# A hybrid encoder block: streamed tiles moved by 32 bytes, decay tables filled up to 128 rows, and two heads' score products in turns

## The chip, the core and the metric

The kernel runs on one core of one Trainium2 chip. The metric is the device time of one execution in microseconds (us). The median of the runs shown is what a change is measured against. TensorE does the products, VectorE (DVE), ScalarE (ACT) and GpSimd (POOL) the elementwise work, SyncE (SP) issues most transfers.

## What is computed

One layer of a two-branch encoder block over 1024 tokens of 1024 features, in float32. The part that the change touches is the chunked SSD scan: 16 heads of 64 channels, 8 chunks of 128 tokens, forward and backward.

```python
h = _rms_norm(x, norm_mix_pre); proj = h @ w_in
z, xbc, dt_raw, u = jnp.split(proj, split_at, axis=-1)
y_ssd = _ssd_mixer(z, xbc, dt_raw, ...)          # two directions of _ssd_scan, then gate and norm
y_s5 = _s5_mixer(u, ...)                          # S5 scan, then g * sigmoid(g @ glu_w + glu_b)
mix = jnp.concatenate([y_ssd, y_s5], axis=-1) @ w_out
x = x + _rms_norm(mix, norm_mix_post)
h = _rms_norm(x, norm_ffn_pre)
f = (jax.nn.silu(h @ w_gate) * (h @ w_up)) @ w_down
x = x + _rms_norm(f, norm_ffn_post)
...
# in _ssd_scan, per head and chunk (l, s: tokens of a chunk)
decay = jnp.exp(jnp.where(lower, a_cum[..., :, None] - a_cum[..., None, :], -jnp.inf))
scores = jnp.einsum("bclgn,bcsgn->bcgls", cc, bc)
y_diag = jnp.einsum("bcgrls,bcsgrp->bclgrp", scores[:, :, :, None] * decay, xdt)
y_off = jnp.einsum("bclgn,bcgrpn,bcgrl->bclgrp", cc, states_in, jnp.exp(a_cum))
```

## The kernel before

The large products are done in float32r halves: an operand is split into a high and a low part, and three products (high by high, high by low, low by high) are added in PSUM. In the profile a product is written `out<-streamed,stationary`. The stages, in the order of the program: norm and the input projection (streamed `hTh`, `hTl`), the S5 branch, the GLU of the S5 branch (streamed `gh`, `glo`, function `gemm`, L271), the SSD branch, the output projection (streamed `ohi`, `olo`, L1123), the gate and up products of the feed-forward in Winograd's form (streamed `B` and `T`, L1535), the down product (streamed `dop`, L1839).

The SSD branch works on eight units `q`, each of two heads; a unit has two halves `hf` of four chunks. It is written as a generator, and pieces of it are let in between the pieces of the GLU and of the output projection (`fill_with`). Outside the stretches with a manual schedule, priorities set the order in which a scheduler places instructions on each engine; each engine then runs its list in order. In one half of a unit:

- `u3`: for each head and direction the exponents of the decay are made on TensorE. A product of `ra` (streamed) with `la` (stationary), both of 16 rows (L971), and a product of `neg` with `idr` of 128 rows that adds the mask (L972) fill one PSUM bank; ACT takes the exponential into `E`. Two more products of `ra` with `efs`, over 8 rows (L978), give the factors `EF`. Eight units by two halves by four make 64 products of 16 rows, and there are 32 of 8 rows.
- `u4`: `M` of a head is the sum of its two `E` times the scores `SL` (L990, L991). The products of `M` with `X` (L994, float32, 64 stationary columns) put head 0 in partitions 0 to 63 of `yd` and head 1 in 64 to 127: four products of head 0, then four of head 1. Each is two passes in the profile. DVE and POOL then add the part from the chunk states (L1008, L1011 to L1013).

The first rows of `la` and the last of `ra` are constants made once by `ssd_tables`; the other eight rows are loaded for each unit (`unit_loads`). `t16`, `r16`, `dtT` and `xT` take turns in two buffers of the tag `xT`.

SBUF is given out from both ends. In the kernel before, the tiles of the pools on the right side start 32 bytes past a multiple of 64, and so do those behind `dvec` on the left: `gh`, `glo`, `ohi`, `olo`, `T`, `ra`, `neg`, `M`, `CT`, `Xw` among the streamed ones. `hTh`, `hTl`, `B` and `dop` start at multiples of 64.

Of the kernel before, what the change touches and what calls it, by code (L numbers as in the profile page):

```python
# [18 lines left out]
def _ap(t, off, dims):  # L19
    """A free-dimension pattern over all partitions of tile t."""  # L20
    return bass.AP(tensor=t.tensor, offset=t.offset + off, ap=[list(t.ap[0])] + [list(d) for d in dims])
# [109 lines left out]
def hymba_block(ctx, tc, P, out, dbg=None, upto=99):  # L131
# [69 lines left out]

# [1 line left out]
    ident = const.tile([128, 128], F32, name="ident")  # L203
# [13 lines left out]

# [1 line left out]
    wst = ctx.enter_context(tc.tile_pool(name="wst", bufs=2))  # L219
# [31 lines left out]
    def ensure(i):  # L251
        """splits of the weight blocks up to i, and the load of the one after"""
        for j in range(min(i + 1, len(stream))):
            if j in wt:
                continue
            fetch(j)
            raw, n = raws[j], stream[j][1]
            hi = wst.tile([128, 8, n], F32R, tag="whi", name="whi")
            lo = wst.tile([128, 8, n], F32R, tag="wlo", name="wlo")
            with hpri("s0" if j < 2 else "sA" if j < XBC0 else "sB" if j < GL0 else "sG" if j < FF0 else "sF"):  # L260
                act.copy(hi, raw)  # L261
                (pool if ("0" if j < 2 else "A" if j < XBC0 else "X" if j < Z0 else "Z" if j < GL0 else "G" if j < FF0 else "F") in KN['pl'] else dve).tensor_tensor(lo, raw, hi.bitcast(F32), op=SUB)  # L262
            wt[j] = (hi, lo)
        if i + 1 not in (GL0, FF0):
            fetch(i + 1)
# [7 lines left out]

# [1 line left out]
    # the normed input, transposed, in exact halves; one pool for each half of the tokens  # L275
    hst, hTh, hTl = [None, None], [None, None], [None, None]
# [59 lines left out]
    def turn_chunk(c):  # L336
        """one chunk of the first half, turned; two channel tiles of two chunks share a bank"""
        if c % 2 == 0:
            tq[c // 2] = [(pacc if c and k < 3 else ptmp)() for k in range(4)]
        for k in range(8):  # L340
            o = 256 * (k % 2) + 128 * (c % 2)
            pe.transpose(tq[c // 2][k // 2][:, o:o + 128], xts[c][:, 128 * k:128 * k + 128], ident)
# [21 lines left out]

# [1 line left out]
    nsm = [0]  # L366
# [37 lines left out]
    def s5_prep():  # L404
# [52 lines left out]
        ensure(3)  # L457
        # BB = k*b, packed [-BBi, BBr, BBi]; C packed [Cr, -Ci, -Cr]
        bre = pp.tile([128, 1024], F32, tag="n1", name="bre")
# [49 lines left out]

# [1 line left out]
    @pri("lu")  # L511
# [5 lines left out]
    def pw4(t, d, n0, nn, g0, ng):  # L517
        """powers n0.. of (group, power), all states, spread over 16 channels"""
        v = t[:, n0 - 1:n0 - 1 + nn, 64 * d + g0:64 * d + g0 + ng].rearrange("p n g -> p g n")
        return v.unsqueeze(3).to_broadcast([128, ng, nn, 16])  # L520
# [80 lines left out]
    def dt_block():  # L601
        # rows 0-31 from the high halves of the weight, rows 32-63 from the low ones
        dt_t = io.tile([64, 1024], F32, tag="io", name="dt_t")
# [8 lines left out]

# [1 line left out]
    @pri("rec")  # L614
    def rec_step(j):
        def at(k, swap=False):
            # forward block k, backward block 127 - k
            return _ap(SH, 64 * k + (32 if swap else 0),
# [15 lines left out]

# [1 line left out]
    cps, W0s, Us_ = {}, {}, {}  # L636
# [60 lines left out]
    def w0_load(b):  # L697
        """block-Toeplitz taps of 4 groups, 240 columns apart: rows (7 - step, channel), columns (step, channel)"""
        W0 = W0s[b] = wst.tile([128, 960], F32, tag=("whi", "wlo")[b % 2], name="W0")
# [37 lines left out]

# [1 line left out]
    Gs = {}  # L739
# [10 lines left out]
    def restack(b):  # L750
        """states of 4 groups that enter each block, (part, state) on partitions"""
        while len(AHs) < 2:
# [35 lines left out]

# [1 line left out]
    @pri("dtp")  # L790
    def dt_prep():
# [47 lines left out]
        act.activation(cd[:, 1].rearrange("p c h -> p c h"), tot[:, 1, ::-1, :], AF.Exp)  # L839
        # rows of the running sums, and of log(dt) less them, in exact halves  # L840
        ln = sper.tile([128, 2, 8, 16], F32, tag="d2", name="ln")
# [16 lines left out]

# [1 line left out]
    def transposes(dst, src):  # L860
        """dst [128, 8, 128] <- the 8 column blocks of src [128, 1024], transposed"""
        for q in range(2):
# [21 lines left out]
    def ssd_tables():  # L884
# [9 lines left out]
        for i in range(2):  # L894
            la.append(un.tile([16, 8, 128], F32R, name=f"la{i}"))
            ra.append(un.tile([16, 8, 128], F32R, name=f"ra{i}"))
            act.copy(la[i], t)
            act.copy(ra[i], r)
        for d in range(2):
            for hh in range(2):  # L900
                act.copy(efs[:, d, 64 * hh:64 * hh + 64], t[:, 4 * d + hh, 0:64])
        act.copy(idr, ident)
# [18 lines left out]
    def unit(q, ssum):  # L921
# [15 lines left out]
        with hpri("u2"):  # L937
            # chunk states, then the states that enter each chunk
            Sn = un.tile([128, 2, 7, 128], F32, tag="Sn", name="Sn")
# [22 lines left out]
        for hf in range(2):  # L962
            with hpri("u3"):
# [11 lines left out]
                for d in range(2):  # L975
                    EF = un.tile([128, 512], F32, tag="EF", name="EF", bufs=2)
                    xp = ptmp()
                    pe.matmul(xp, efs[0:8, d, :], Rr[0:8, 4 * hf:4 * hf + 4, :].rearrange("p c l -> p (c l)"), start=True, stop=True)  # L978
                    act.activation(EF, xp, AF.Exp)
# [4 lines left out]
            with hpri("u4"):  # L984
                yd = ptmp()
                for hh in range(2):
                    E = Es[hh]
                    M = un.tile([128, 4, 128], F32, tag="M", name="M", bufs=2)
                    Mv = M.rearrange("p c l -> p (c l)")
                    pd(f"m{hf}{hh}").tensor_tensor(Mv, E[:, 0], E[:, 1], op=ADD)  # L990
                    dve.tensor_tensor(Mv, Mv, SL[:, g, 4 * hf:4 * hf + 4, :].rearrange("p c l -> p (c l)"), op=MUL)  # L991
                    for j in range(4):
                        c = 4 * hf + j
                        pe.matmul(yd[64 * hh:64 * hh + 64, 128 * j:128 * j + 128], X[:, c, 64 * hh:64 * hh + 64], M[:, j, :],  # L994
                                  start=True, stop=True)
# [42 lines left out]

# [1 line left out]
    early = {}  # L1040
# [35 lines left out]

# [1 line left out]
    w_out = P["w_out"]  # L1078
# [10 lines left out]
    def load_wout(r0, n, cb):  # L1089
        """n pairs of 128-row tiles of w_out from row r0 on, columns 512*cb.."""  # L1090
        r = []
# [11 lines left out]
    def load_cat(c0, n, l, own=False):  # L1103
        """halves of 4 channel tiles of the mixed outputs at step l: (part, tile, token)"""
        r = []
# [50 lines left out]

    # ================= order of work =================
    ps0 = pacc()
# [46 lines left out]
    act.copy(vec2, pv[:, 0:128])  # L1205
    # the sigmoids of the GLU and of the convolution's SiLU are taken as (1 + tanh(v / 2)) / 2
    dve.tensor_scalar_mul(vec2[:, R_B:R_CW + 60], vec2[:, R_B:R_CW + 60], 0.5)
# [110 lines left out]
    cd = sper.tile([128, 2, 8, 16], F32, name="cd")  # L1318
    dvec = sper.tile([128, 8], F32, name="dvec")
    CT = sper.tile([128, 2, 1024], F32, name="CT")  # L1320
    Bt = sper.tile([128, 8, 2, 128], F32, name="Bt")
# [70 lines left out]

    efs = un.tile([16, 2, 128], F32R, name="efs")
    idr = un.tile([128, 128], F32R, name="idr")
# [56 lines left out]

# [1 line left out]
    # pairs of 128 hidden channels; the seven products of half blocks (Winograd's form)  # L1453
    NF = 22
# [84 lines left out]
    def block(p, f, hf, acc, n, m):  # L1539
        """one block of the results of both matrices, and from them the hidden channels"""  # L1540
        if m == 0:
# [52 lines left out]

# [1 line left out]
    tl = []  # L1596
# [177 lines left out]

# [1 line left out]
    # blocks: the halves of the tokens, of each pair of tiles of hidden channels, of the columns  # L1776
    ffst = newstack()
# [174 lines left out]
```

## Time and profile before

| | |
|---|---|
| median of three runs | 1748.66 us (1744.92 to 1759.22) |
| profiled execution | span 1758.7 us; the run of 1759.22 us is the one nearest to it, 0.5 us above |
| busy share of the span | PE 92%, PE weight loads 73%, DVE 72%, ACT 41%, POOL 33% |
| chain that ended last | PE 47%, DVE 6%, POOL 5%, DMA 5%, issue 3%, ACT 2% |
| PE busy from 740 to 1000 us | 253.70 of 260 us |
| PE busy from 1105 to 1526 us | 413.55 of 421 us |

The page adds the time in which an engine has an instruction in work. A matmul is pipelined, so its own duration is longer than the distance to the start of the next one; the pace of TensorE is read from starts in the timeline. A row of the timeline that ends in x24 holds 24 instructions in a row on that engine, and the next row's start ends it.

### The profile page before, as it was taken

Reading aid. Unit: us, or ns where it says so; the run is one execution under the profiler, and the core shown is the slowest. Engines: PE = TensorE matmul, PEld = TensorE weight load, DVE = VectorE, ACT = ScalarE, POOL = GpSimd, SP = SyncE. Lnnn points to the kernel's source line nnn. Section 1 sums busy time; section 2 is a strip of 40 time slices with the busy share of each in tenths; the row PEclk is TensorE's granted clock in tenths of the full one; section 3 lists DMA queues with packets and bytes.
Section 4 is the critical chain, followed back from the end, with each engine's and each line's share of the span. In section 5 each row is a group of like instructions: output and inputs, shape, how many; then the busy total and the mean of one; then the engine's idle time right before and its main releaser. Section 6 shows DMA issues by size and latency. Waiting matters only on the chain.

```text
span 1758.7 us, 22308 instructions
## 1 busy us (share of the span) xinstructions
PE 1609.5 (92%) x7980; PEld 1277.1 (73%) x7980; DVE 1273.6 (72%) x2012; ACT 717.5 (41%) x1182; POOL 573.2 (33%) x510
## 2 busy tenths in 40 slices
PE   7999999789767979999999987899999999999897
PEld 6777788577665756667666765688888888787686
DVE  7445589999652667776556579888877887669877
ACT  6344622211877545443333245323222222355352
POOL 2111122164220120111111057655445555319612
PEclk9999999899889889999999998899999999999999
DMA  6643344334767647767458893322223321492235
GB/s 179 160 119 104 119 140 139 123 99 116 168 156 199 189 146 239 227 212 238 155 157 266 246 302 120 120 102 96 96 96 128 112 97 49 169 362 70 93 102 180
DMA packets 250146, 272.13 MB, mean 155 GB/s; under 512 B 29403, under 2 KB 190675, under 8 KB 250035
## 3 DMA queue, kind: packets, MB, share of 16 engines
q1 hardware_dynamic: 224659, 216.48, 40.3%
q0 software_dynamic: 12896, 33.83, 6.1%
q10 hardware_dynamic: 12480, 20.39, 3.2%
q8 instruction: 63, 1.03, 0.2%
q14 instruction: 48, 0.39, 0.1%
HBM read 185.76 MB, written 84.84 MB: 154 GB/s over the span
## 4 chain that ended last, share of the span: by engine, by line
PE 47%; DVE 6%; POOL 5%; DMA 5%; issue 3%; ACT 2%; SPq 0%; POOLq 0%; DVEq 0%; ACTq 0%
PE acc L1535 13%; PE ptmp L1535 9%; PE acc L1123 7%; PE acc L271 4%; PE ptmp L1839 3%; POOL wd L1806 3%; PE acc L1839 2%; PE ptmp L971 2%; PE ptmp L1008 1%; PE ptmp L946 1%; PE ptmp L994 1%; PE ptmp L972 1%; DMA m<-m_d 1%; DVE dop L1821 1%; DMA cat<-ch_d 1%
## 5 line engine op out<-in xcount | busy, mean ns | idle before, releaser
L1123 PE MATMUL acc<-ohi,cat 128*128 128x512 f32 x512 | 182.9, 423 | 8.8 <-DMA cat<-ch_d 7.0
L271 PE MATMUL acc<-hTh,whi 128*128 128x512 f32 (+1 forms) x456 | 180.3, 396 | 8.6 <-ACT whi L261 8.2
L271 PE MATMUL acc<-hTh,wlo 128*128 128x512 f32 (+1 forms) x456 | 179.1, 393 | 2.1 <-POOL wlo L262 2.1
L271 PE MATMUL acc<-hTl,whi 128*128 128x512 f32 (+1 forms) x456 | 179.7, 394 | 0.7 <-DVE hTl L331 0.6
L1518 DVE TENSOR_TENSOR wop<-rawp,wop 128x512 fp32r<-128x512 f32 x120 | 137.4, 1146 | 17.7 <-ACT wop L1517 16.5
L1535 PE MATMUL ptmp<-T,wop 128*128 128x512 f32 x528 | 129.8, 401 | 7.1 <-DVE T L1692 4.8
L1535 PE MATMUL acc<-T,wop 128*128 128x512 f32 x528 | 129.9, 401 | 3.7 <-DVE T L1692 3.7
L1123 PEld LDWEIGHTS acc<-ohi,cat 128*128 128x128 f32 x512 | 100.7, 198 | 40.0 <-issue 8.1
L1535 PEld LDWEIGHTS ptmp<-T,wop 128*128 128x128 f32 x528 | 101.0, 192 | 32.1 <-DVE T L1692 5.1
L1535 PE MATMUL acc<-B,wop 128*128 128x512 f32 x528 | 124.2, 391 | 0.0
L1839 PE MATMUL ptmp<-dop 128*128 128x512 f32 x528 | 120.7, 389 | 2.8 <-DVE dop L1821 2.8
L262 POOL TENSOR_TENSOR wlo<-raw,whi 128x1024 fp32r<-128x1024 f32 x20 | 49.9, 2496 | 221.4 <-ACT whi L261 221.3
L1535 PEld LDWEIGHTS acc<-T,wop 128*128 128x128 f32 x528 | 100.8, 191 | 29.0 <-DVE T L1692 4.5
L1839 PEld LDWEIGHTS ptmp<-dop 128*128 128x128 f32 x528 | 98.9, 188 | 24.0 <-DVE dop L1821 3.4
L1535 PEld LDWEIGHTS acc<-B,wop 128*128 128x128 f32 x528 | 99.0, 188 | 21.7
L271 PEld LDWEIGHTS acc<-hTh,whi 128*128 128x128 f32 x456 | 87.1, 191 | 27.4 <-ACT whi L261 8.6
L1123 PE MATMUL acc<-olo,cat 128*128 128x512 f32 x256 | 105.9, 414 | 0.0
L1550 ACT ACTIVATE cg<-cg 128x512 f32<-128x512 f32 x44 | 27.8, 632 | 188.0 <-DVE cg L1548 188.0
L1556 POOL TENSOR_TENSOR cg<-cg 128x512 f32<-128x512 f32 x44 | 61.7, 1403 | 128.3 <-DVE cg L1551 127.6
L271 PEld LDWEIGHTS acc<-hTh,wlo 128*128 128x128 f32 x456 | 86.8, 190 | 21.8 <-POOL wlo L262 4.1
L1517 ACT CAST wop<-rawp 128x512 fp32r<-128x512 f32 x120 | 70.8, 615 | 77.7 <-POOL rawp L1492 50.2
L1839 PE MATMUL acc<-dop 128*128 128x512 f32 x396 | 95.7, 398 | 7.4 <-DVE dop L1821 4.8
(360 smaller groups left out, 3617.0 us busy)
## 6 DMA issues: line engine op xcount, KB each, us to landing
ff_d<-cg POOLq DMA_DIRECT2D x77, 256.0 KB, 2.3
da<-ff_d SPq DMA_DIRECT2D x35, 512.0 KB
raw<-in_w_in_dram SPq DMA_DIRECT2D x28, 512.0 KB
cat<-ch_d SPq DMA_DIRECT2D x48, 256.0 KB
cat<-cl_d SPq DMA_DIRECT2D x48, 256.0 KB
wd<-in_w_down_dram SPq DMA_DIRECT2D x44, 256.0 KB
rawp<-in_w_gate_dram SPq DMA_DIRECT2D x10, 1024.0 KB
rawp<-in_w_up_dram SPq DMA_DIRECT2D x10, 1024.0 KB
```

The costliest lines, as they stand in the source:

```text
L262: (pool if ("0" if j < 2 else "A" if j < XBC0 else "X" if j < Z0 else "Z" if j < GL0 else "G" if j < FF0 else "F") in KN['pl'] else dve).t ...
L271: pe.matmul(ps, a[:, k, :], b[:, k, sl], start=(k == 0 and n == 0), stop=(k == 7 and n == 2))
L946: pe.matmul(t[:, 256 * s + 128 * d:256 * s + 128 * d + 128], Bt[:, c, g, :], Xw[:, d, c].rearrange("p h e -> p (h e)"), start=True, stop=True)
L971: pe.matmul(xp, L[:, 4 * d + 2 * hf + hh, :], rv, start=True, stop=False)
L1123: pe.matmul(ps, c[:, a, k % 4, :], b[:, k % 2, :], start=(k == 0 and n == 0), stop=(k == n_ - 1 and n == 2))
L1517: act.copy(t[:, 0], src)
L1518: dve.tensor_tensor(t[:, 1], src, t.bitcast(F32)[:, 0], op=SUB)
L1535: pe.matmul(ps, a[:, ai, k, :], b[:, bi, k, :], start=(k == 0 and q == 0), stop=(k == 3 and q == 2))
L1550: act.activation(cg[:, 0], cg[:, 0], AF.Silu)
L1556: pool.tensor_tensor(dst, a, b, op=op)
L1806: pool.tensor_tensor(w[:, o], w[:, a], w[:, b], op=SUB)
L1839: pe.matmul(ps, t[:, 0, a, 128 * j:128 * j + 128], t[:, 1, b, :], start=(q == 0 and n == 0), stop=(q == NP - 1 and n == 2))
```

## The change

Three things are done. Two tiles of eight floats (`edge`, `edge2`) are allocated, one as the first pool of the right side and one behind `dvec`; what is given out after them moves by 32 bytes, and the streamed tiles named above start at multiples of 64. `la`, `ra` and `efs` get 128 partitions; GpSimd fills them with zeros before the constant rows are copied in, and L971 and L978 run over 128 rows. The products of `M` with `X` go chunk by chunk, one of head 0 and one of head 1 in turns, after both `M` are made.

```diff
@@ long-lived pools
+    edge = ctx.enter_context(tc.tile_pool(name="edge", bufs=1, side="right"))
+    pool.memset(edge.tile([128, 8], F32, name="edge"), 0.0)
...
@@ ssd_tables
-            la.append(un.tile([16, 8, 128], F32R, name=f"la{i}"))
-            ra.append(un.tile([16, 8, 128], F32R, name=f"ra{i}"))
-            act.copy(la[i], t)
-            act.copy(ra[i], r)
+            la.append(un.tile([128, 8, 128], F32R, name=f"la{i}"))
+            ra.append(un.tile([128, 8, 128], F32R, name=f"ra{i}"))
+            pool.memset(la[i].bitcast(F32), 0.0)
+            pool.memset(ra[i].bitcast(F32), 0.0)
+            act.copy(la[i][0:16], t)
+            act.copy(ra[i][0:16], r)
+        pool.memset(efs.bitcast(F32), 0.0)
         for d in range(2):
             for hh in range(2):
-                act.copy(efs[:, d, 64 * hh:64 * hh + 64], t[:, 4 * d + hh, 0:64])
+                act.copy(efs[0:16, d, 64 * hh:64 * hh + 64], t[:, 4 * d + hh, 0:64])
...
@@ unit, u3
-                    pe.matmul(xp, efs[0:8, d, :], Rr[0:8, 4 * hf:4 * hf + 4, :].rearrange("p c l -> p (c l)"), start=True, stop=True)
+                    pe.matmul(xp, efs[:, d, :], rv, start=True, stop=True)
...
@@ unit, u4
                 yd = ptmp()
+                Ms = []
                 for hh in range(2):
                     E = Es[hh]
                     M = un.tile([128, 4, 128], F32, tag="M", name="M", bufs=2)
+                    Ms.append(M)
...
-                    for j in range(4):
-                        c = 4 * hf + j
-                        pe.matmul(yd[64 * hh:64 * hh + 64, 128 * j:128 * j + 128], X[:, c, 64 * hh:64 * hh + 64], M[:, j, :],
+                for j in range(4):
+                    c = 4 * hf + j
+                    for hh in range(2):
+                        pe.matmul(yd[64 * hh:64 * hh + 64, 128 * j:128 * j + 128], X[:, c, 64 * hh:64 * hh + 64], Ms[hh][:, j, :],
                                   start=True, stop=True)
...
@@ order of work
     dvec = sper.tile([128, 8], F32, name="dvec")
+    pool.memset(sper.tile([128, 8], F32, name="edge2"), 0.0)
...
-    efs = un.tile([16, 2, 128], F32R, name="efs")
+    efs = un.tile([128, 2, 128], F32R, name="efs")
```

On TensorE, at the first half of unit 5 (`M` of head 0 and of head 1 by their numbers, all products into one bank), before:

```order
L1123 MATMUL acc_7068<-ohi_6932,cat_7065 128x512 x2
L1123 MATMUL acc_7068<-olo_6933,cat_7065 128x512
L1123 MATMUL acc_7068<-ohi_6932,cat_7065 128x512
L994 MATMUL ptmp_7096<-M_7097,X_6973 64x128 x4
L994 MATMUL ptmp_7096<-M_7104,X_6973 64x128 x4
L1008 MATMUL ptmp_7112<-CT_4066,Sn_6991 128x128 x3
```

On TensorE at the same place in the changed kernel:

```order
L1135 MATMUL acc_7080<-ohi_6944,cat_7077 128x512 x2
L1135 MATMUL acc_7080<-olo_6945,cat_7077 128x512
L1135 MATMUL acc_7080<-ohi_6944,cat_7077 128x512
L1006 MATMUL ptmp_7108<-M_7109,X_6985 64x128
L1006 MATMUL ptmp_7108<-M_7112,X_6985 64x128
```

The two last rows come four times in turns before L1020 follows, so the eight products stand in the same place between the same neighbours, and the two heads alternate. Twelve of the sixteen halves are so; in the other four the heads were apart. On TensorE at the first of those (unit 0, first half; `gh`, `glo` are the GLU's), before:

```order
L271 MATMUL acc<-gh,wlo 128x512
L994 MATMUL ptmp<-M,X 64x128 x4
L1008 MATMUL ptmp<-CT,Sn 128x128 x7
L971 MATMUL ptmp<-ra_5036,la_5035 128x512
L972 MATMUL ptmp<-neg,idr 128x512
L994 MATMUL ptmp<-M,X 64x128 x4
L271 MATMUL acc<-gh,whi 128x512
L271 MATMUL acc<-glo,whi 128x512
```

On TensorE at the same place in the changed kernel:

```order
L275 MATMUL acc<-gh,wlo 128x512
L1006 MATMUL ptmp<-M,X 64x128
L1020 MATMUL ptmp<-CT,Sn 128x128 x7
L979 MATMUL ptmp<-ra_5043,la_5042 128x512
L980 MATMUL ptmp<-neg,idr 128x512
L275 MATMUL acc<-gh,whi 128x512
L275 MATMUL acc<-glo,whi 128x512
L275 MATMUL acc<-gh,wlo 128x512
L1006 MATMUL ptmp<-M,X 64x128 x7
```

Of the eight products one stays where it was and seven stand where the second head's were, three GLU products later; in both kernels they stand in two groups.

On ACT, where the tables of the SSD branch are copied (during the first GLU blocks), before:

```order
L1056 CAST gh<-graw 128x1024
L902 CAST idr<-ident 128x128
L901 CAST efs<-t_5017 16x64 x4
L1056 CAST gh<-graw 128x1024
L897 CAST la_5035<-t_5017 16x1024
L897 CAST la_5039<-t_5017 16x1024
L898 CAST ra_5036<-r_5026 16x1024
L898 CAST ra_5040<-r_5026 16x1024
L1067 ACTIVATE sg<-acc,vec_423 128x512
```

On ACT at the same place in the changed kernel:

```order
L1068 CAST gh<-graw 128x1024
L910 CAST idr<-ident 128x128
L1068 CAST gh<-graw 128x1024
L904 CAST la_5042<-t_5024 16x1024
L904 CAST la_5048<-t_5024 16x1024
L905 CAST ra_5043<-r_5033 16x1024
L905 CAST ra_5049<-r_5033 16x1024
L909 CAST efs<-t_5024 16x64 x4
L1079 ACTIVATE sg<-acc,vec_428 128x512
```

The four copies into `efs` moved behind those into `la` and `ra`. `dtT`, which took the buffer of `t16` before, now takes that of `r16`. On POOL five fills of zeros (four of 128x1024, one of 128x256) stand between its last issue for the S5 taps and its first for `rr_d`.

## Rows read from the trace of the kernel before

**Rows 1.** The page's chain of work that ended last, by engine.

```profile
PE 47%; DVE 6%; POOL 5%; DMA 5%; issue 3%; ACT 2%; SPq 0%; POOLq 0%; DVEq 0%; ACTq 0%
```

**Rows 2.** Windows: stretch, its length, busy per engine, granted clock, DMA share.

```profile
740.00:1000.00 260.00, 253.70 (x1217) 184.44 (x1216) 158.69 (x280) 92.37 (x129) 35.83 (x24) 0.96 0.67 210
1000.00:1105.00 105.00, 84.97 (x357) 68.17 (x358) 87.56 (x109) 49.38 (x111) 62.56 (x44) 0.89 0.65 208
1105.00:1526.00 421.00, 413.55 (x1774) 334.19 (x1772) 336.23 (x351) 124.78 (x217) 220.63 (x199) 0.99 0.29 99
```

**Rows 3.** Waits of TensorE from 740 to 1000 us: total, times, longest.

```profile
PE ptmp L946 <- DVE Xw L933: 6.2, 4, 2.2
```

**Rows 4.** Timeline of TensorE in the gate and up stage: start, us.

```profile
1157.06 5.64 PE L1535 MATMUL acc<-B,wop 128*128 128x512 f32 x24
1162.55 5.78 PE L1535 MATMUL ptmp<-T,wop 128*128 128x512 f32 x24
1168.16 5.76 PE L1535 MATMUL acc<-T,wop 128*128 128x512 f32 x24
```

**Rows 5.** Groups by line and form: count, busy us, mean ns, idle before.

```profile
L1123 PE MATMUL acc<-ohi,cat 128*128 128x512 f32 x512 | 182.9, 423 | 8.8 <-DMA cat<-ch_d 7.0 <-ACT ohi L1086 1.5 <-DVE m L1152 0.3
...
L1535 PE MATMUL ptmp<-T,wop 128*128 128x512 f32 x528 | 129.8, 401 | 7.1 <-DVE T L1692 4.8 <-ACT T L1689 2.3
...
L1123 PE MATMUL acc<-olo,cat 128*128 128x512 f32 x256 | 105.9, 414 | 0.0
...
L271 PE MATMUL acc<-gh,wlo 128*128 128x512 f32 x128 | 53.9, 421 | 0.9 <-DVE wlo L262 0.9
```

**Rows 6.** Timeline of TensorE in the output projection, first group.

```profile
750.18 0.63 PE L1123 MATMUL acc<-ohi,cat 128*128 128x512 f32 x2
...
750.88 0.63 PE L1123 MATMUL acc<-ohi,cat 128*128 128x512 f32 x2
```

**Rows 7.** Chain of work in order of time, down product: start, us, what.

```profile
1556.48 19.05 PE acc L1839 x84
```

**Rows 8.** Timeline of TensorE around one 16-row product, unit 3, second half.

```profile
801.80 0.40 PE L1123 MATMUL acc<-ohi,cat 128*128 128x512 f32 x1
802.12 0.49 PE L971 MATMUL ptmp<-ra,la 16*128 16x512 f32 x1
802.54 0.50 PE L1123 MATMUL acc<-ohi,cat 128*128 128x512 f32 x1
802.88 0.39 PE L972 MATMUL ptmp<-neg,idr 128*128 128x512 f32 x1
803.11 0.40 PE L1123 MATMUL acc<-olo,cat 128*128 128x512 f32 x1
```

**Rows 9.** Lines L971 and L978 alone: count, ns least/median/most, first and last start.

```profile
L971 PE MATMUL ptmp<-ra,la x64: 488/491/735, 630.9 to 977.7; 16*128 16x512 f32 x64
...
L978 PE MATMUL ptmp<-ra,efs x32: 392/491/791, 635.7 to 980.4; 8*128 8x512 f32 x32
```

**Rows 10.** Timeline of TensorE: the two heads' products of one half, and L552.

```profile
146.42 2.27 PE L552 MATMUL ptmp<-U,bm 128*64 128x128 f32 x32
148.62 1.09 PE L544 MATMUL ptmp<-ident,bp 128*128 128x128 f32 x8
...
755.41 1.58 PE L994 MATMUL ptmp<-M,X 128*64 128x128 f32 x16
756.92 1.83 PE L1008 MATMUL ptmp<-CT,Sn 128*128 128x128 f32 x14
```

**Rows 11.** Timeline of DVE ahead of that half: both heads' `M`.

```profile
750.68 0.69 DVE L991 TENSOR_TENSOR M<-M,SL 128x512 f32<-128x512 f32 x1 [1.18 <-POOL M L990]
...
754.28 0.68 DVE L991 TENSOR_TENSOR M<-M,SL 128x512 f32<-128x512 f32 x1
```

**Rows 12.** The tables: chain of work, SP's issues, a fill on POOL.

```profile
572.59 1.90 ACT ra L898 x2
...
572.62 0.49 SPq L793 DMA_DIRECT2D dtT<-dt_d  x1
...
L208 POOL MEMSET tri_ge<- 128x128 f32 x1 | 0.2, 205 | 0.0
```

## The prediction

> **What bounds the kernel now.** I read the chain that ended last first: TensorE holds 47% of it, and DVE, POOL and DMA some 5% each [rows 1]. Then I cut the span into stages. In the stretch that holds SSD units 2 to 7 and the first group of the output projection, and in the gate and up stage, TensorE is busy for 253.70 of 260 us and 413.55 of 421 us, while DVE is at 61% and 80% [rows 2]. The waits of TensorE in the first of these come to 6.2 us in 260 [rows 3]. So TensorE's list is the bound in both, and the question is what TensorE's time is made of. Its busy time does not say that, since a matmul's own length overlaps the next one's; the distance between starts does. Three things stand out there.
>
> First, pace. A block of 24 products that stream `B` takes 1162.55 − 1157.06 = 5.49 us, the next block, which streams `T`, 5.61 us [rows 4]. Same shape, same stationary tile; `B` starts at a multiple of 64 bytes and `T` 32 bytes past one. In the output projection three products take 750.88 − 750.18 = 0.70 us, 233 ns each [rows 6], streaming `ohi` and `olo`, which are off as well. Products of `dop`, which is not, run at 19.05 / 84 = 227 ns [rows 7].
>
> Second, the 16-row product. It starts 0.32 us after the product before it, takes 0.42 us to the next start, and that next one, of 128 rows, takes 0.34 us; only the one behind it is back at 0.23 us [rows 8]. No engine is named as waited for: TensorE does not run the two row counts into one another, on either side.
>
> Third, the two heads' products. One half takes 756.92 − 755.41 = 1.51 us for 16 passes; L552, which already changes column halves from product to product, has 32 passes in 148.62 − 146.42 = 2.20 us, 1.10 us for 16, and a change of bank lies inside that [rows 10].
>
> **The alignment.** Gate and up: 1056 products stream `T` (the row of 528 and one like it) [rows 5], 44 blocks of 24; each saves 5.61 − 5.49 = 0.12 us [rows 4]: 5.3 us, with nothing else waiting there. Output projection: 512 + 256 products [rows 5] at 233 instead of 227 ns: 4.6 us. GLU: 128 in the row and two groups like it, 384 [rows 5], by 6 ns: 2.3 us, of which I take 1.5, since the first blocks run beside the wait for the SSD tables. The float32 products have no pair of rows that differ in this alone: between 0 and 2 us, and I take 1. Sum 12.4 us. If these 5 to 7 ns came from something that `T` and `ohi` share other than their place, the term is 0.
>
> **The rows.** Four starts, from 801.80 to 803.11, take 1.31 us [rows 8]; at 0.23 us each they would be 0.92, so one excursion costs 0.39 us. There are 64 + 32 = 96 such products, all between 630 and 981 us [rows 9]; a few follow one another directly and share the edges, so I count 92 full ones and 4 at their own excess of 0.42 − 0.23 = 0.19 us: 36.6 us. This is the largest term. Its lower bound, if a 128-row product with zeros kept the edges, is 0; if only its own pace became normal, 96 × 0.19 = 18 us. I take the upper value, because L972 with its 128 rows stands among the 128-row products of L1123 at 0.23 us to its successor [rows 8], and the changed L971 has its shape and type.
>
> The Trainium skill, "TensorE: Matmul & The Clock Gate", section "LDWEIGHTS (loading the stationary operand)", says that the number of rows does not change the time of a weight load, and its section "Why this matters for your kernels" that a product of 32 rows takes as long as one of 128; by that alone this term would be 0 and the sum about 14 us. "TensorEngine Tiling (Array Packing)", section "Key Properties", says that a change of tiling mode drains TensorE; by that the whole 36.6 us go. The trace agrees with the second: the excess lies at the changes of shape, before and behind.
>
> **The turns.** 1.51 − 1.10 = 0.41 us a half [rows 10], 16 halves: 6.6 us. Both kernels have 20 groups of these products, so the edges of the groups stay. The bound below is negative: the group now needs both `M` after its first product. At the half shown DVE has the first `M` ready at 751.37 and the second at 754.96, and TensorE comes at 755.41 [rows 10, 11]. The slack is 0.45 us, and TensorE will come earlier: two to six excursions of 0.39 us lie between the exponents and the group, while ACT and DVE start earlier by nearly as much. I book 5 us of new waits for all 16 halves and the `Xw` waits of [rows 3] together (0 to 20). Behind a waiting group on TensorE stand L1008 and the output projection; DVE waits for `yd`.
>
> **The tables.** Five fills on POOL: a 128x128 one is 0.205 us [rows 12], so 1024 columns are at most 1.64 and five at most some 7 us by that rate. POOL has nothing else there, and ACT reaches `la` only after the second `gh`; I take 0. Without that cover ACT, and `dtT` behind it, would be late by up to those 7 us. What does move is `dtT`. Before, SP issues it at 572.62, when ACT has finished with `t16` and turns to `ra` at 572.59 [rows 12]; now it waits for the two `ra` copies, 1.90 us later. The chain of work holds these copies, so +1.9 us; behind `dtT` on SP's queue stand the first `xT`, the GLU's stores and its next weight loads, late by the same, and TensorE's products for the step sizes wait for `dtT`. The `efs` copies put four short casts ahead of the GLU's next activation; TensorE waits for this transfer at that time anyway, 0. The `edge` fills are 0.1 us on an idle POOL, 0.
>
> **Sum.** 12.4 + 36.6 + 6.6 − 1.9 − 5 = 48.7 us. Against the profiled execution this is a span of 1758.7 − 48.7 = 1710 us; against the median of the runs, which lies 10 us below that execution, **1700 us**. The float32 and clock terms lean to the fast side: TensorE's clock was granted at 0.96 over the 260 us [rows 2], which is 0.04 × 2 × 260 = 21 us at the half level (1.2 of 2.4 GHz), costing about 10 us, and fewer stalls may give back part of it. If half of it came back and no wait was new, the gain would be 48.7 + 5 + 5 = 59 us, and with the stated upper ends of the alignment terms 62: 1687 us. I let the range begin at 1683.
>
> **Rivals.**
> *The gain turns into waits.* With 48 us less to do in the SSD stretch, TensorE waits for DVE's `M` and `Xw`, and the clock falls. For it speaks the stretch from 1000 to 1105 us: TensorE busy for 85 of 105 us and the clock at 0.89 [rows 2]. At 0.89 instead of 0.96 the 260 us hold 36 us more at the half level, which lose 18 us; with 8 us more of waits the gain is 48.7 − 26 = 23 us: 1726 us. Against it: DVE is at 61% there and mostly waits for TensorE itself.
> *The zero rows do not help*: the edges come from something in `la`, `ra` other than the row count. Then 48.7 − 36.6 + 5 = 17 us: 1732 us. Against it: the excess lies before and behind the product as well as in it [rows 8]. This is what the Trainium skill's "TensorE: Matmul & The Clock Gate", quoted above on row counts, would give alone.
> *Slower, through the joint wait.* If DVE, serving the output projection and the convolution between the two `M`, kept the second one 3.6 us behind the first (754.28 − 750.68) [rows 11] and TensorE came as early as the first, each half would lose 3.6 us, 16 halves 58 us: more than the 48.7 + 5 us of the terms without waits; with the clock's 18 us, 1748.7 − 53.7 + 58 + 18 = 1771 us. The point from which it decides is a mean wait of 53.7 / 16 = 3.4 us at the group. Against it: today the slack is positive, and TensorE gains at most six excursions, 2.3 us, on DVE within a half.
>
> **How the numbers follow.** A measurement of this kernel can tell about 1%, 17 us, from no change. Forecast 1700 us, chance 0.78; waits and clock (1726) 0.11; zero rows idle (1732) 0.07; slower (1771) 0.04. The first two lie over 1% below the median; of the third half falls within 1%: faster 0.92, same 0.04, slower 0.04. The range reaches from 1683 to the waits case, 1726, and leaves out the last two.
>
> **What would show it.** Right: `T` blocks at 5.49 us or less; L971 and L978 at 0.23 us to the next start, with no longer start before or behind them; the two heads' 16 passes in about 1.1 us; units 2 to 7 in some 225 us instead of 260. Wrong: the changed L971 still at 0.42 us, TensorE waits for DVE's `M` of over 1 us a half, or a granted clock below 0.9 in that stretch.

## The result and the profile after

The changed kernel took 1711.66 us (median of 4 runs, 1704.13 to 1714.9); the kernel before took 1748.3 us beside it (4 runs, 1744.92 to 1759.22). The medians are 36.6 us apart. The ratio on record, which is not the quotient of the two medians, is 0.9757 with an interval of 0.9723 to 0.9791; by it the gain is 42.5 us (36.5 to 48.4), and all gains below are reckoned from such ratios. Timed again later (e9 below) the ratio was 0.9712, 50.6 us. The forecast was 1700 us within 1683 to 1726.

First the page's chain by engine, as in [rows 1], and the windows that hold the same work as the first two of [rows 2], found by their first and last products; the columns are those of [rows 2].

```profile
PE 40%; DVE 10%; DMA 8%; issue 3%; POOL 3%; ACT 2%; SPq 0%; DVEq 0%; POOLq 0%; ACTq 0%
```

```profile
726.00:951.00 225.00, 216.19 (x1216) 179.03 (x1214) 158.16 (x275) 89.22 (x129) 37.11 (x24) 0.98 0.76 239
951.00:1061.00 110.00, 87.65 (x360) 70.45 (x359) 87.81 (x111) 49.47 (x111) 62.84 (x44) 0.86 0.64 204
```

The work that took 260 us now takes 225, as the prediction had it. The granted clock in this stretch is 0.98, and 0.98 again in e9, where the kernel before had 0.96 [rows 2], and 0.97 in a second trace (e7). So an estimated 9 us (0.02 × 2 × 225) lie at 1.2 GHz where 16 to 21 us did, and by this estimate 3 to 6 of the 35 us come back through the clock. TensorE's share of the chain fell from 47% to 40%, and DVE's and DMA's rose; but the same row of e1, whose time is within 1% of before, has PE 42% and DVE 8%, so this row proves little by itself.

Then the timeline of TensorE where a product of `ra` and `la` stands alone in the output projection, the place that answers to [rows 8].

```profile
852.30 0.40 PE L1135 MATMUL acc<-ohi,cat 128*128 128x512 f32 x1
852.53 0.40 PE L979 MATMUL ptmp<-ra,la 128*128 128x512 f32 x1
852.77 0.40 PE L1135 MATMUL acc<-ohi,cat 128*128 128x512 f32 x1
853.00 0.39 PE L980 MATMUL ptmp<-neg,idr 128*128 128x512 f32 x1
853.23 0.39 PE L1135 MATMUL acc<-olo,cat 128*128 128x512 f32 x1
```

Every start is 0.23 us behind the one before it. The 0.32, 0.42 and 0.34 us of [rows 8] are gone on all three sides of the product; its own length fell from a median of 491 ns [rows 9] to 392:

```profile
L979 PE MATMUL ptmp<-ra,la x64: 388/392/500, 626.0 to 930.7; 128*128 128x512 f32 x64
```

The two heads' products of one half, as in [rows 10], and DVE's two `M` ahead of them, as in [rows 11]:

```profile
848.44 1.09 PE L1006 MATMUL ptmp<-M,X 128*64 128x128 f32 x16
849.47 1.83 PE L1020 MATMUL ptmp<-CT,Sn 128*128 128x128 f32 x14
```

```profile
844.37 0.69 DVE L1001 TENSOR_TENSOR M<-M,SL 128x512 f32<-128x512 f32 x1 [1.13 <-POOL M L1000]
844.98 0.68 DVE L1000 TENSOR_TENSOR M<-E 128x512 f32<-128x512 f32 x1
845.70 0.69 DVE L1001 TENSOR_TENSOR M<-M,SL 128x512 f32<-128x512 f32 x1
```

The 16 passes take 1.03 us instead of 1.51; all the stretches of these products together, 20 of them in either kernel, take 19.6 us (20.1 in e9) instead of 26.3. The second `M` is there at 846.39 and TensorE comes at 848.44, so the joint wait has 2 us of slack here.

Gate and up, as in [rows 4]:

```profile
1107.33 5.66 PE L1548 MATMUL ptmp<-T,wop 128*128 128x512 f32 x24
1112.82 5.62 PE L1548 MATMUL acc<-B,wop 128*128 128x512 f32 x24
1118.27 5.67 PE L1548 MATMUL ptmp<-T,wop 128*128 128x512 f32 x24
```

The `T` block takes 1112.82 − 1107.33 = 5.49 us, where it took 5.61. The median of all 44 `T` blocks is 5.51 us, a little over the number forecast; that of the 32 `B` blocks is 5.49 (5.48 before), so the 5.45 of this one is not typical.

Last, the waits of TensorE: two rows from 726 to 951 us, the stretch that answers to [rows 3], and two from 951 to 1061 us.

```profile
PE ptmp L954 <- DVE Xw L941: 7.8, 4, 3.6
PE ptmp L1006 <- DVE M L1001: 0.9, 3, 0.3
```

```profile
PE acc L1135 <- DMA cat<-ch_d: 7.6, 3, 3.8
...
PE acc L1135 <- DVE m L1164: 2.3, 1, 2.3
```

The wait for `cat` is not new (7.0 us in [rows 5]); that for `m` is, 2.3 us here and in e9 where it was 0.3.

Along the program the difference grows like this. The first product of `M` and `X` comes at 631.3 us instead of 638.0, the last one at 937.3 instead of 986.0 (first and last starts of that line's 128 products), the first of gate and up at 1023.0 instead of 1066.9. The 6.7 us at the first of these are no gain: in e7 the kernel before is there at 627.1. From the first product of `M` and `X` to the last it is 306.1 us (303.4 in e9) instead of 348.0 (345.6 in e7), so 40 to 45 us are won within the SSD stretch. From there to gate and up it is 85.6 us (83.6 in e9) instead of 80.9 (83.3 in e7): the seven traces without the tables of 128 rows lie between 80.6 and 83.3, the five with them between 83.6 and 85.6, so some 3 us are given back. The span is 45.5 us shorter, and 34.3 us against e7.

### The profile page after: what moved, and what is told of

Read it like the earlier page. It is cut to its first block, busy times and chain, and to the rows that moved or that the text cites. A ratio compares the mean times of both kernels' runs of the same rounds, so it can differ in the third digit from the quotient of the medians.

```text
span 1713.2 us, 22320 instructions
## 1 busy us (share of the span) xinstructions
PE 1560.2 (91%) x7980; PEld 1272.9 (74%) x7980; DVE 1268.8 (74%) x2012; ACT 712.4 (42%) x1182; POOL 579.3 (34%) x517
## 3 DMA queue, kind: packets, MB, share of 16 engines
q8 instruction: 63, 1.03, 0.3%
## 4 chain that ended last, share of the span: by engine, by line
PE 40%; DVE 10%; DMA 8%; issue 3%; POOL 3%; ACT 2%; SPq 0%; DVEq 0%; POOLq 0%; ACTq 0%
PE acc L1548 13%; PE ptmp L1548 9%; PE acc L1135 4%; PE ptmp L1852 4%; PE acc L1852 3%; DVE dop L1834 2%; PE acc L275 2%; DMA m<-m_d 2%; POOL wd L1819 1%; PE ptmp L954 1%; DMA m_d<-m 1%; PE ptmp L1020 1%; DMA cat<-ch_d 1%; PE ptmp L1006 1%; DMA graw<-g_d 1%
## 5 line engine op out<-in xcount | busy, mean ns | idle before, releaser
L1135 PE MATMUL acc<-ohi,cat 128*128 128x512 f32 x512 | 176.3, 411 | 11.0 <-DMA cat<-ch_d 7.6
L1834 DVE TENSOR_TENSOR dop<-da,dop 128x512 fp32r<-128x512 f32 x77 | 76.7, 996 | 38.9 <-ACT dop L1833 38.9
```

What stands on the lines that cost most here:

```text
L1135: pe.matmul(ps, c[:, a, k % 4, :], b[:, k % 2, :], start=(k == 0 and n == 0), stop=(k == n_ - 1 and n == 2))
L1834: dve.tensor_tensor(t[:, k, 1], src, t.bitcast(F32)[:, k, 0], op=SUB)
```

## The experiments

All start from the kernel before, unless said otherwise. Ratios are to the kernel before, run beside.

**e1_align: the two edge tiles alone.**

```diff
+    pool.memset(edge.tile([128, 8], F32, name="edge"), 0.0)
+    pool.memset(sper.tile([128, 8], F32, name="edge2"), 0.0)
```

> Only the two tiles that move the others by 32 bytes; tables of 16 rows and head after head as before. By the prediction's theory (the streamed tile's own place decides) T, ohi, olo and gh run at 227 ns and the kernel gains 12 us: 1736 us. By the rival (the distance between the streamed tile and the stationary tile that is loaded meanwhile decides, and 64 bytes are left of it) they run at 229 to 230 ns, as in the changed kernel, and the gain is 8 us or less: 1740 us.

Measured: 1750.18 us over 10 runs, ratio 0.998 (0.995 to 1.001): 3.5 us, at most some 9. The 12.4 us of my sum are outside. The trace says a part of why: `T` went from 233.6 to 229.3 ns from start to start, not to the 227 of `dop` [rows 7].

**e2_rows: the tables of 128 rows alone.**

```diff
-            la.append(un.tile([16, 8, 128], F32R, name=f"la{i}"))
+            la.append(un.tile([128, 8, 128], F32R, name=f"la{i}"))
+            pool.memset(la[i].bitcast(F32), 0.0)
-            act.copy(la[i], t)
+            act.copy(la[i][0:16], t)
...
-                    pe.matmul(xp, efs[0:8, d, :], Rr[0:8, ...], ...)
+                    pe.matmul(xp, efs[:, d, :], rv, ...)
```

(`ra` and `efs` likewise.)

> Only the tables with zero rows up to 128. By the prediction's theory (a change of the array's shape costs 0.39 us on the way in and out) 36.6 us less the 1.9 us of the late step-size transfer and some waits: 1716 us, the products of ra with la at 0.23 to 0.24 us to the next start. By the rival that much of it turns into waits of TensorE for Xw, M and transfers: 1728 us or more, with over 10 us of new waits between 560 and 1000 us.

Measured: 1714.23 us, ratio 0.9803 (0.9773 to 0.9833), 34.5 us (29 to 40). This is nearly the whole change. My term, 36.6 less 1.9 for the later `dtT`, lies inside the interval. In the trace it is 309.8 us from the first product of `M` and `X` to the last, instead of 348.0 and 345.6.

**e3_turns: the score products taking turns, alone.**

```diff
-                    for j in range(4):
-                        c = 4 * hf + j
-                        pe.matmul(yd[64 * hh:64 * hh + 64, ...], X[...], M[:, j, :], ...)
+                for j in range(4):
+                    c = 4 * hf + j
+                    for hh in range(2):
+                        pe.matmul(yd[64 * hh:64 * hh + 64, ...], X[...], Ms[hh][:, j, :], ...)
```

> Only the two heads' products in turns. By the prediction's theory 0.41 us a half, 6.6 us in all: 1742 us, 16 passes in 1.0 to 1.1 us. By the rival (the wait for both M eats it) no gain or a loss: 1748 us or more, with TensorE waiting for M before these products.

Measured: 1749.92 us over 10 runs, ratio 0.9979 (0.9955 to 1.0002), 3.7 us (0 to 7.9). TensorE's timeline shows the group at its new length:

```profile
764.55 1.09 PE L997 MATMUL ptmp<-M,X 128*64 128x128 f32 x16
765.57 1.16 PE L1011 MATMUL ptmp<-CT,Sn 128*128 128x128 f32 x8
```

1.02 us instead of 1.51; all these products together take 17.9 us instead of 26.3, so 8.4 us are gained in this trace. TensorE waited 7.5 us for `Xw` from 740 to 1000 us, where [rows 3] had 6.2 and e7 6.8, so little of it goes into that wait. The times can't tell 6.6 from 3.7.

**e4_rows64: the tables with 64 rows.** This asks whether the gain of e2 comes from more rows or from no change of shape.

```diff
-            la.append(un.tile([128, 8, 128], F32R, name=f"la{i}"))
+            la.append(un.tile([64, 8, 128], F32R, name=f"la{i}"))
```

> Tables with zero rows up to 64 instead of 128. If the cost is one of changing the array's shape, 64 rows are still another shape than 128 and nothing is gained: about 1749 us, 0.42 us to the next start. If it is one of the count of rows, a part of it goes: 0.33 us to the next start and some 18 us gained.

Measured: 1750.32 us in one run, no gain that it can tell (the 19 runs of the kernel before beside it: 1745.88 to 1767.22). TensorE's timeline:

```profile
827.20 0.39 PE L1126 MATMUL acc<-olo,cat 128*128 128x512 f32 x1
827.51 0.50 PE L974 MATMUL ptmp<-ra,la 64*128 64x512 f32 x1
827.94 0.51 PE L975 MATMUL ptmp<-neg,idr 128*128 128x512 f32 x1
828.28 0.63 PE L1126 MATMUL acc<-ohi,cat 128*128 128x512 f32 x2
```

0.31, 0.43 and 0.34 us: the 64-row product pays what the 16-row one paid in [rows 8]. It is the change of row count between neighbours that costs, not how few rows there are. The kernel before shows the same where two products of 8 rows follow one another:

```profile
748.53 0.51 PE L972 MATMUL ptmp<-neg,idr 128*128 128x512 f32 x1
748.96 0.73 PE L978 MATMUL ptmp<-ra,efs 8*128 8x512 f32 x2
749.62 0.50 PE L1123 MATMUL acc<-ohi,cat 128*128 128x512 f32 x1
749.95 0.39 PE L1123 MATMUL acc<-olo,cat 128*128 128x512 f32 x1
```

The two take 0.66 us to the next start, not twice the 0.42 of a lone one: the edges are paid once for both. This is what the Trainium skill, "TensorEngine Tiling (Array Packing)", section "Key Properties", says of a change of tiling mode; here its cost is 0.39 us for one excursion and back.

**e5_mult128: the changed kernel with edge tiles of 24 floats instead of 8**, so that the streamed tiles stand at multiples of 128 bytes.

```diff
-    pool.memset(edge.tile([128, 8], F32, name="edge"), 0.0)
+    pool.memset(edge.tile([128, 24], F32, name="edge"), 0.0)
-    pool.memset(sper.tile([128, 8], F32, name="edge2"), 0.0)
+    pool.memset(sper.tile([128, 24], F32, name="edge2"), 0.0)
```

> The changed kernel with both edge tiles of 24 floats instead of 8, so that every streamed float32r tile and its stationary tile start at multiples of 128. If the distance between the two decides, T, ohi, olo and gh go from 229.5 to 227 ns: 2208 products by 2.5 ns, 5 us, 1706 us. If the streamed tile's place at a multiple of 64 is all that counts, nothing changes: 1711 us and 229 to 230 ns.

Measured: 1699.5 us over 6 runs, ratio 0.9711 (0.9671 to 0.975). `T` blocks are at 5.44 us, below the 5.49 that I had reckoned with.

**e6_left32: the other side moved.** A tile of 8 floats behind `vecs` moves everything on the left by 32 bytes, the stationary tiles among it; `T`, `ohi` and `gh` stay where they were, 32 bytes past a multiple of 64.

```diff
     vecs = const.tile([128, 8], F32, name="vecs")
+    pool.memset(const.tile([128, 8], F32, name="shift"), 0.0)
```

> The kernel before with one tile of 8 floats more at the left end: everything on the left moves by 32 bytes, the right side stays. Streamed hTh, B and dop now start 32 bytes past a multiple of 64, with their stationary tiles at the same distance as before; T, gh and ohi stay where they are and their stationary tiles come 64 bytes from them instead of 96. If the streamed tile's place decides, hTh, B and dop fall to 233 ns (3084 products by 6 ns, 18 us slower: 1766 us) and T stays at 233 ns. If the distance decides, hTh, B and dop stay at 227 ns and T goes to 229 to 230 ns: 6 to 8 us faster, 1741 us.

Measured: 1753.26 us in one run beside 1753.41; the 1741 us of the distance is not seen, but one run can't exclude it. TensorE's timeline decides between the two:

```profile
1157.66 5.67 PE L1536 MATMUL ptmp<-T,wop 128*128 128x512 f32 x24
1163.17 5.66 PE L1536 MATMUL acc<-T,wop 128*128 128x512 f32 x24
1168.67 5.65 PE L1536 MATMUL acc<-B,wop 128*128 128x512 f32 x24
```

`T` blocks of 5.51 and 5.50 us, as in the changed kernel, with `T` itself unmoved, and the products of `hTh`, `B` and `dop`, moved by 32 bytes, keep their 227 to 228 ns. The streamed tile's own place is not what counts.

**e7_before: the kernel before, unchanged, a second trace**, to see how much of a difference between two traces is no difference of kernels.

> The kernel before, unchanged, for a second trace. The first one's execution was 10 us above the median. If that excess lies in the stretch of the SSD units, as half-clock time or waits, the changed kernel's gain over a usual execution is smaller there than the sum says; if it lies elsewhere (the S5 stage, the end), the sum holds stage by stage and only the base was high.

Measured: 1749.16 us, span 1747.5 against 1758.7. Of these 11 us, 7.7 lie between the first S5 output product and the first product of `gh`, 107.6 us instead of 115.3, and 3.5 behind the step sizes, before the first product of `Xw`. The SSD stretch (256.3 and 255.3 us from the first `ohi` to the last `M`) and gate and up (456.0 and 454.2) hardly differ, so hardly any of it lies where the change saves.

**e8_align128: the kernel before with the 24-float edge tiles alone.**

```diff
+    pool.memset(edge.tile([128, 24], F32, name="edge"), 0.0)
+    pool.memset(sper.tile([128, 24], F32, name="edge2"), 0.0)
```

> The kernel before with one edit alone: the two edge tiles of the change, widened from 8 to 24 floats, so that the streamed tiles stand at multiples of 128 bytes, as their stationary tiles do. Tables and score products stay as before. Distance theory (what counts is the distance from the streamed tile to the stationary one of the next product, taken in 128 bytes: 0 is 227 ns from start to start, 64 is 229.5, 96 is 233.6): about 1950 products go from 233.6 to 227.4 ns, 12 us, so 1738 to 1742 us or a ratio of 0.993, and T, ohi and gh each at 227 to 228.5 ns in the trace. Place theory (a start at a multiple of 64 bytes is enough): the same as the 8-float tiles alone, which had a ratio of 0.998, so 1748 to 1751.

Measured: 1744.99 us over 11 runs, ratio 0.9938 (0.9918 to 0.9957): 10.9 us, three times what the 8-float tiles gave. The timeline of gate and up:

```profile
1141.63 5.60 PE L1539 MATMUL ptmp<-T,wop 128*128 128x512 f32 x24
1147.07 5.60 PE L1539 MATMUL acc<-B,wop 128*128 128x512 f32 x24
1152.51 5.60 PE L1539 MATMUL ptmp<-T,wop 128*128 128x512 f32 x24
```

All blocks are at 5.44 us. The distance theory gave 12. (`B`, at distance 0 in both kernels, went from 5.48 to 5.44 us too, which the distance doesn't account for.) In the SSD stretch of the profiled execution none of it is seen, but there the granted clock was 0.93 instead of 0.96 [rows 2]:

```profile
740.00:1000.00 260.00, 252.84 (x1198) 186.59 (x1197) 151.37 (x270) 87.15 (x121) 35.38 (x24) 0.93 0.66 205
```

That is 0.03 × 2 × 260 = 16 us more at 1.2 instead of 2.4 GHz, which by this estimate cost 8 us in this one execution.

**e9_after and e10_mult128: the changed kernel and that of e5 once more, on one chip.** No edit.

> The changed kernel as it is, timed again beside the next run on the same chip. Ratio to the kernel before 0.972 to 0.979, as in its first runs; T at 229.3 ns from start to start.

> The changed kernel with edge tiles of 24 floats again, on the chip that runs the changed kernel beside it. Distance theory: some 1950 products go from 229.5 to 227.4 ns, 4 us, so 4 to 5 us below the changed kernel of the same call. Rival: the 12 us between the first runs of these two kernels (1711.7 and 1699.5) are all from the alignment, then 10 to 14 us below. Rival place theory: no difference, and the 12 us were the spread from call to call.

Measured: 1704.21 us, ratio 0.9712 (0.9686 to 0.9738), and 1702.86 us, ratio 0.9695 (0.9668 to 0.9723), 6 runs each. The wider tiles give the lower ratio both times, but the intervals overlap; the 12 us between the first runs of the two came down to 1.4. In the traces, gate and up is 447.1 us instead of 451.0, so 4 us are shown there; that they reach the end of the program is not.

## Why the prediction was right

**The rows: right, in mechanism and size.** 36.6 us forecast; 34.5 in e2, and the timeline after shows the edges gone on both sides. The rival that the zero rows don't help (1732 us) falls with e2, and e4, the same edit with 64 rows, shows that a smaller table would not have helped. Only the four products that follow another directly were booked wrongly: such a pair costs 0.40 us together, not 0.19 us more than one, which is 0.8 us in all. On the Trainium skill's "TensorE: Matmul & The Clock Gate", section "Why this matters for your kernels", which I had set against this term: that a product of few rows is no faster holds here (491 ns against 392), but a row count that differs from the neighbours' is dearer.

**The alignment: right in sign, wrong in its rule, and so too large.** The step that failed: "`B` starts at a multiple of 64 bytes and `T` 32 bytes past one", from which I let every streamed tile at a multiple of 64 reach 227 ns. I had compared the streamed tiles with each other, and never looked at where the stationary tiles stand. With the addresses that the program gives the tiles, the traces order themselves by one number: the start of the streamed tile less that of the stationary tile, modulo 128. The mean from start to start of 128x512 products with 128 rows (pairs less than 260 ns apart, at full clock):

```
distance   kernel      products (streamed, stationary mod 128)     mean ns
0          before      dop (0, 0)                                  227.1
0          e6          dop (32, 32)                                227.1
0          before      ohi (96, 96)                                227.7
0          e5, e8      T (0, 0)                                    226.8
64         e1, after   T (64, 0)                                   229.3
64         e6          T (96, 32)                                  229.3
96         before      T (96, 0)                                   233.6
96         before      gh, ohi (96, 0)                             233.6, 233.7
```

The change moves the streamed tiles by 32 bytes, which takes most of them from 96 to 64, and saves 4.3 ns of a possible 6.6. The pairs (96, 96) and (32, 32) exclude the place of either tile alone. In these rows a product's own stationary tile and the next one, loaded meanwhile, stand alike, so which of the two counts is not shown; in some 70 pairs of the changed kernel, and again in e9, they differ (streamed 64, own 0, next 64), and there it is 232 ns, which neither distance gives. A quarter of the `ohi` and `olo` products, 192 whose `cat` stands at 96 too, were at 227 ns from the start, and I had counted them among the 768 to win. By the program's addresses 1898 products stand at 96 in the kernel before. At 4.3 ns each the change's shift is worth 8 us of my 12.4, and e1's time shows only 3.5 (at most 9); at 6.6 ns, with the distance at 0, it is 12.5, and e8 measures 10.9. What e1's missing 4 us went into is not settled. Its profiled execution gains in gate and up (451.1 us) and is no shorter in the SSD stretch, and neither are those of e6 and e8. From the first `ohi` to the last `M` the granted clock was 0.95, 0.95 and 0.94 in these three, 0.96 and 0.97 in the two traces of the kernel before; by an estimate (the difference times 256 us) that costs 3 to 5 us in e1. Why the clock was lower there, no run shows.

**The turns: right in mechanism, and in size by the traces.** 26.3 us of these products became 19.6 and 20.1, waits among them included: 6.2 to 6.8 us against 6.6 forecast. The time of e3 alone gives 3.7 us (0 to 7.9) and does not confirm the size. The negative bound did not come about: 0.9 us of waits for `M` in three halves (1.4 in e9), and 2 us of slack in the half shown. The slower rival (1771 us), which wanted 3.4 us at each group, falls with it.

**The tables: a third of the price or less.** `dtT` did move behind the `ra` copies, and the chain now passes through them and the transfer. But from the first `gh` product to the step sizes it is 23.2 us (23.1 in e9) against 22.6 (22.8 in e7): 0.3 to 0.6 us instead of 1.9, since TensorE had waited for the first `xT` there before. The fills on POOL take 3.9 us and end at 566.4, before ACT turns to `la` at 566.8.

**The new waits: about half of the 5 us booked, and as much elsewhere.** Waits for DVE's `Xw` rose from 6.2 us [rows 3] (6.8 in e7) to 7.8 (7.3 in e9), and `M` adds 0.9 (1.4). What the prediction did not have is the 2.3 us for `m` behind the stretch; with it the total is near 5 us again, which is luck. The clock did not fall, 0.98 instead of 0.96 in the stretch and 0.86 instead of 0.89 behind it, where e7 has 0.87 and e9 too, so the rival of waits and clock (1726 us) did not come either. A few us came back through the clock, as the prediction allowed for without booking them; that the fewer stalls did it is not shown.

**The sum.** Alone, the three parts give 34.5 + 3.5 + 3.7 = 41.7 us; together 42.5 and, in the later runs, 50.6. They add up as far as the intervals tell, each some 4 to 5 us to either side; 48.7 lies just above the first interval for the whole (36.5 to 48.4) and inside the second (46.1 to 55.2). The 12 us between the first median and 1700 are in part the spread, since the second median of the same kernel is 1704.21. The traces put the over-booked alignment, 4 to 9 us, first among the terms that were too large; the tables and the clock set off some of it, so that the total came so near is not all merit. Two side sums of the prediction don't come out: without the rows' term the sum is 12 us with the booked waits and 17 without them, not 14, and the terms for the fast end make 60.5 us, not 62. The forecast does not hang on either.

## What to carry to other kernels

Read a product's cost from the distance between starts, with its neighbours on both sides: a small odd-shaped product among large ones can cost more at its edges than in itself, and filling it up with zero rows can be free. When two streams of the same shape run at different paces, write down the addresses of everything that the engine reads, the stationary tiles too, before naming one of them the cause. Take the base of a forecast from more than one trace where there is one: 11 us of the 1758.7 were no part of the kernel.

## What the runs showed of the hardware

TensorE's pace depends on where the streamed tile and the stationary tile stand to one another: 227 ns at a distance of 0 modulo 128 bytes, 229.3 at 64 and 233.6 at 96, for float32r products of 128 rows and 512 columns. The Trainium skill, "TensorE: Matmul & The Clock Gate", section "Step-by-step: what each phase is for", has two read ports, one for the streamed operand and one for the weight load, and says that the load takes no read bandwidth from the running product; the traces here show products 1% and 3% longer by the places of the two tiles. What makes it so, and whether it is the load, no run here shows.

A 64-row product among 128-row ones costs the same 0.39 us as a 16-row one, and the edges lie half outside the product's own row; a second 8-row product directly behind the first does not pay them again.
